# Two trunk layers in one launch: the opening modulation ahead of the tokens, and two projection tiles by turns

## The chip, the cores and the metric

The kernel runs on one core of one Trainium2 chip. TensorE (PE) does matmuls and transposes, VectorE (DVE), ScalarE (ACT) and GpSimd (POOL) do the work on vectors, SyncE (SP) issues the transfers in order. The metric is the device time of one launch in microseconds.

## The reference

One layer of a hybrid backbone is run for 1024 sample tokens and 256 prompt tokens that share all weights. Only the first part matters here:

```
mod = silu(cvec) @ w_mod + b_mod                 # (1024 x 6144)
sh1, sc1, g1, sh2, sc2, g2 = split(mod, 6)
h = rmsnorm(x, g_pre1) * (1.0 + sc1) + sh1
p = h @ w_in                                     # four head groups A, B, C, D
ya, yb, yc = short_conv(p[A]), gla(p[B], s0), chunk_mlp(p[C])
yd = hyena(p[D])                                 # row_conv3, then two long convolutions by FFT
x = x + g1 * rmsnorm(concat(ya, yb, yc, yd) @ w_out, g_post1)
x = x + g2 * rmsnorm(swiglu(rmsnorm(x, g_pre2) * (1 + sc2) + sh2), g_post2)
```

The filters of the long convolutions come from a small sine network (`filter_mlp`) and are taken to the frequency domain (`filter_spectra`).

## The kernel before

The 1280 tokens are three chunks: `CH = [(0, 512), (512, 512), (1024, 256)]`. Every large product runs as three products of a high and a low part: `mm3` does high weights by high tokens (L90), low tokens (L91) and low weights by high tokens (L92).

The opening, in `run`, makes the normalised, modulated and transposed tokens: `hh[n]` and `hl[n]`, the two parts of chunk n, eight blocks (`kt`) of 128 rows each.

- `mod_first(part)` is a generator with one step per 512 KB tile of w_mod: the transfer (L122) into one of seven buffers `s4`, which the `w_in` tiles and their parts use too, then four 32-column matmuls (L132) into one PSUM bank. With the fifth tile comes the bias (L129). Behind the eighth: copy (L135), two transposes (L138), copy (L140) and `mod_apply` (L378, L379), which writes the scale `sv` and the shift `bv`. Part 0 serves blocks 0 to 3 of every chunk, part 1 blocks 4 to 7. A buffer is free when the matmuls that read it are done, and the transfer into it waits for that on SP, with all transfers behind it.
- `norm1_rows(n)` loads 128 rows at a time (L388), squares them on ACT (L1609) and scales them by the root (L97, L98, L392).
- `chunk_hT(n, ..., kts)` transposes four such tiles per block (L401; two for chunk 2) into one of four banks `pm`, and `to_hT` empties it: ACT writes `hh` (L199), then DVE (L201) or ACT (L203) writes a full copy into one of two `tmp`, and POOL or DVE subtracts (L204) into `hl`.
- `load_w(ti)` loads a 512 KB tile of w_in (L83); ACT casts it to the high part (L65), DVE subtracts to the low part (L66). `later`, the second and third round of the modulation (L161, L164), takes a step with each call.
- `proj_d` makes six projection tiles (`ti`) for the long convolution, each for three chunks: 24 matmuls into a bank `pg`, a convolution (`conv3`: ACT L226, DVE L229 and L230), transposes into phases (L614, L618), a copy (L620) and a store to `xg` (L622).

Behind these come the products of `mixer_d` (`p`, L662 to L751, the FFTs), with projections of other head groups as fill, and `mixer_b`, whose chain begins with L924: two matmuls per chunk, ACT L925, L938, L940 over all chunks, and DVE's scans L944, L949. A scheduler sets the order on each engine from the program's order, its estimates and the buffers; so a change at the front moves rows far behind.

Of the kernel before, what the change touches and what calls it, by code (L numbers as in the profile page):

```python
# [20 lines left out]
KT = D // P  # L21
# [20 lines left out]
class Builder:  # L42
# [193 lines left out]
    def run(self):  # L236
        tc, nc, a = self.tc, self.nc, self.a
        with ExitStack() as ctx:
# [49 lines left out]
            with banks() as self.psm, sub("fl", side="right") as fl:  # L288
                h2 = fl.tile([P, T], F32R, name="h2")
                with sub("xs", side="right") as xs, sub("flm", side="right") as flm:  # L290
                    mod = [self.mod_first(0), self.mod_first(1)]
                    mlp = self.filter_mlp(flm, h2)
                    next(mod[0])
                    self.consts(const)
                    next(mlp)
                    for _ in range(2):
                        next(mod[0])
                    with tc.issue_after(self.mark.ins):
                        x = [self.norm1_rows(0, xs)]
                    for _ in mlp:  # L300
                        pass
                    for _ in mod[0]:
                        pass
                    self.chunk_hT(0, x[0], 0, self.pm, range(4))
                    next(mod[1])
                    with tc.issue_after(self.mark.ins):
                        x.append(self.norm1_rows(1, xs))
                    self.chunk_hT(1, x[1], 0, self.pm, range(4))
                    for _ in range(3):
                        next(mod[1])  # L310
                    with tc.issue_after(self.mark.ins):
                        x.append(self.norm1_rows(2, xs))
                    self.chunk_hT(2, x[2], 0, self.pm, range(4))
                    for _ in mod[1]:
                        pass
                    with tc.issue_after(self.mark.ins):
                        w = self.load_w(0)
                    for n in range(3):
                        self.chunk_hT(n, x[n], 0, self.pm, range(4, KT))
                self.later = itertools.chain(self.mod_round(1), self.mod_round(2))  # L320
                with sub("flk", side="right") as flk:
                    self.filter_spectra(flk, h2)
# [265 lines left out]
    def proj_d(self, first):  # L588
        self.hyconv = self.cst.tile([P, 6, 3], F32, name="hyconv")
        self.nc.sync.dma_start(self.hyconv, self.a["hyconv"])  # L590
        pending = None
        for ti in range(6):
            w = self.load_w(ti) if ti else first
            for n in range(3):
                ps = self.proj_fm(w, n, -1 if n == 1 else 1)
                o = self.pj()
                self.conv3(o, ps, self.hyconv[:, ti, ::-1 if n == 1 else 1], n)
                if pending:
                    self.to_phases(*pending)
                pending = (o, ti, n)  # L600
                if (ti, n) == (5, 1):
                    rows = self.load_w(10)
        self.to_phases(*pending)
        return rows
# [1160 lines left out]
```

## Time and profile before

| | |
|---|---|
| median of 3 runs | 1603.81 us (1602.39 to 1604.59) |
| the profiled execution | 1604.68 us, its span 1602.9 us |
| PE busy | 94% of the span |
| DVE, ACT, POOL busy | 64%, 42%, 25% |
| mean granted clock of PE | 0.974 |

The span is what the trace covers; the rest of the execution's time lies around it. PE is busy nearly throughout except in the opening and in stretches around 240 to 600 us. So what the change is worth is to be read from those stretches, wait by wait.

### The profile page before, as it was taken

What the parts mean: (1) busy time and instruction counts of PE and PEld (TensorE: products, weight loads), DVE (VectorE), ACT (ScalarE), POOL (GpSimd) and SP (SyncE); (2) the same over time, 40 slices, a digit from 0 to 9 for tenths busy, and PEclk for the clock granted to TensorE, in tenths of its full rate; (3) what the DMA queues carried; (4) which work ended last, traced back from release to release, by engine and by line L of the source; (5) the groups of instructions that cost most, each with busy time, mean ns of one, the idle gap of its engine ahead of it and who ended that gap; (6) DMA issues with size and microseconds to landing.
All of it is one profiled execution on the core that took longest, in us unless ns stands there. A gap on an engine that the chain in (4) does not pass through costs nothing.

```text
span 1602.9 us, 23276 instructions
## 1 busy us (share of the span) xinstructions
PE 1500.1 (94%) x8517; PEld 1241.8 (77%) x8517; DVE 1027.6 (64%) x1752; ACT 666.5 (42%) x1218; POOL 399.3 (25%) x406
## 2 busy tenths in 40 slices
PE   5999998889889889998979999999999999999996
PEld 2688877878578667787868888888888887888885
DVE  6776559998278897544766556665566535544467
ACT  5754244554356766555432222222222213433352
POOL 1433216566124665442010110101001000000004
PEclk9899998899999999999989999999999999999998
DMA  9435463442823084561124334343344438755576
GB/s 331 141 113 162 129 219 94 134 145 75 269 77 101 21 266 135 171 224 56 60 83 151 116 112 143 128 141 119 121 135 132 126 103 257 241 178 172 168 245 250
DMA packets 163226, 242.17 MB, mean 151 GB/s; under 512 B 34613, under 2 KB 97407, under 8 KB 162984
## 3 DMA queue, kind: packets, MB, share of 16 engines
q1 hardware_dynamic: 163112, 240.69, 46.1%
q8 instruction: 67, 1.10, 0.3%
q14 instruction: 47, 0.39, 0.1%
HBM read 169.05 MB, written 71.58 MB: 150 GB/s over the span
## 4 chain that ended last, share of the span: by engine, by line
PE 58%; DVE 6%; DMA 3%; ACT 3%; issue 3%; POOL 2%; SPq 0%; DVEq 0%; POOLq 0%; ACTq 0%
PE pg L1381 17%; PE pm L1381 7%; PE pg L1543 7%; PE pm L1543 6%; PE pg L90 4%; PE pg L92 4%; PE pg L91 4%; PE pm L90 3%; PE pm L91 3%; PE pm L92 3%; DMA raw<-w2t 1%; DMA s<-in_wfm 1%; DVE e L1029 1%; DVE qbd L1036 1%; PE pm L401 1%
## 5 line engine op out<-in xcount | busy, mean ns | idle before, releaser
L90 PE MATMUL pg<-hh,s 128*128 128x512 f32 (+1 forms) x432 | 157.6, 366 | 3.9 <-ACT s L65 3.4
L92 PE MATMUL pg<-hh,s 128*128 128x512 f32 (+1 forms) x432 | 154.3, 361 | 6.7 <-DVE s L66 6.7
L66 DVE TENSOR_TENSOR op<-raw,op 128x1152 fp32r<-128x1152 f32 x69 | 93.6, 1357 | 101.2 <-ACT op L65 101.0
L91 PE MATMUL pg<-hl,s 128*128 128x512 f32 (+1 forms) x432 | 155.5, 360 | 0.6 <-POOL hl L204 0.6
L1358 POOL TENSOR_TENSOR sr<-s,s 128x512 f32<-128x512 f32 x20 | 25.8, 1292 | 449.8 <-DVE sr L1356 449.8
L65 ACT CAST op<-raw 128x1152 fp32r<-128x1152 f32 x69 | 80.1, 1161 | 134.2 <-PE pg L1543 67.6
L65 ACT CAST s<-s 128x1024 fp32r<-128x1024 f32 (+2 forms) x67 | 69.6, 1039 | 118.0 <-DMA s<-in_w 82.4
L1543 PE MATMUL pg<-op,op 128*128 128x512 f32 x372 | 115.1, 391 | 1.8 <-DVE op L66 1.8
L98 POOL TENSOR_TENSOR rs<-rs,mhalf 128x1 f32<-128x1 f32 x40 | 29.0, 728 | 351.4 <-DVE rs L97 348.2
L1381 PE MATMUL pg<-b1h,s 128*128 128x512 f32 x320 | 108.4, 400 | 8.1 <-ACT t L1388 8.1
L65 ACT CAST su<-sr 128x512 fp32r<-128x512 f32 x80 | 49.5, 620 | 149.9 <-PE pm L1381 55.5
L66 DVE TENSOR_TENSOR s<-s,s 128x1024 fp32r<-128x1024 f32 (+2 forms) x67 | 86.7, 1295 | 34.7 <-ACT s L65 21.4
L1381 PE MATMUL pg<-hh,su 128*128 128x512 f32 x320 | 107.3, 396 | 0.0
L1543 PE MATMUL pm<-op,op 128*128 128x512 f32 x338 | 104.5, 390 | 0.0
L92 PE MATMUL pm<-hh,s 128*128 128x256 f32 x352 | 99.5, 283 | 0.0
L91 PE MATMUL pm<-hl,s 128*128 128x256 f32 x352 | 99.5, 283 | 0.0
L90 PE MATMUL pm<-hh,s 128*128 128x256 f32 x352 | 99.4, 282 | 0.0
L90 PEld LDWEIGHTS pg<-hh,s 128*128 128x128 f32 x432 | 82.5, 191 | 19.9 <-ACT s L65 4.8
L92 PEld LDWEIGHTS pg<-hh,s 128*128 128x128 f32 x432 | 82.1, 190 | 20.4 <-DVE s L66 7.6
L91 PEld LDWEIGHTS pg<-hl,s 128*128 128x128 f32 x432 | 82.5, 191 | 12.5 <-POOL hl L204 0.9
L1386 DVE TENSOR_TENSOR t<-t,pg 128x512 f32<-128x512 f32 x60 | 41.2, 686 | 75.8 <-PE pg L1381 60.3
L1543 PEld LDWEIGHTS pg<-op,op 128*128 128x128 f32 x372 | 70.0, 188 | 16.8 <-DVE op L66 2.3
(393 smaller groups left out, 4162.7 us busy)
## 6 DMA issues: line engine op xcount, KB each, us to landing
s<-in_wmod SPq DMA_DIRECT2D x48, 512.0 KB, 5.3
raw<-actd SPq DMA_DIRECT2D x75, 320.0 KB, 3.5
s<-in_w SPq DMA_DIRECT2D x44, 512.0 KB, 3.8
actd<-t SPq DMA_DIRECT2D x60, 256.0 KB, 3.6
tmp<-in_w SPq DMA_DIRECT2D x44, 256.0 KB, 3.2
w2t<-tmp SPq DMA_DIRECT2D x44, 256.0 KB, 2.1
raw<-w2t SPq DMA_DIRECT2D x44, 256.0 KB
s<-in_wfm SPq DMA_DIRECT2D x18, 512.0 KB, 5.0
```

The source lines that it names most:

```text
L65: nc.scalar.copy(hi, src)
L66: self.cut = (eng or nc.vector).tensor_tensor(lo, src, hi.bitcast(F32), ALU.subtract).ins
L90: mm(ps, lh, rh, start=start, stop=False)
L91: mm(ps, lh, rl, start=False, stop=False)
L92: self.last = mm(ps, ll, rh, start=False, stop=stop).ins
L98: nc.gpsimd.tensor_tensor(out, out, self.mhalf[:, :cols], ALU.pow)
L401: self.nc.tensor.transpose(ps[:, t * P:(t + 1) * P], x[:, kt * P:(kt + 1) * P], self.ident)
L1029: nc.vector.tensor_tensor(ek[:, :, 0, :], rf, bf[:, :, 0, :], ALU.subtract)
L1358: pt(s3, a1[:, c], a2[:, c], ALU.subtract)
L1381: self.last = mm(ps, l[:, k], r[:, k], start=start and k == 0 and i == 0, stop=stop and k == 3 and i == 2, skip_group_check=True).ins
L1386: add = lambda out, x, y: nc.vector.tensor_tensor(out, x, y, ALU.add)
L1543: mm(ps, l, r, start=start and i == 0, stop=stop and i == 2, skip_group_check=True)
```

## The change

In `run`, both parts of the modulation now stand ahead of all transposes, the first weight tile's load behind them, and chunk 0 gets its eight blocks in one go before chunks 1 and 2. The rows of chunks 1 and 2 are loaded after the first weight tile is asked for. In `proj_d`, tiles 0 and 1 take turns by chunks; for that both weight tiles are held until chunk 2. Every engine has the same instructions as before, in another order.

```diff
                     for _ in mod[0]:
                         pass
-                    self.chunk_hT(0, x[0], 0, self.pm, range(4))
-                    next(mod[1])
-                    with tc.issue_after(self.mark.ins):
-                        x.append(self.norm1_rows(1, xs))
-                    self.chunk_hT(1, x[1], 0, self.pm, range(4))
-                    for _ in range(3):
-                        next(mod[1])
-                    with tc.issue_after(self.mark.ins):
-                        x.append(self.norm1_rows(2, xs))
-                    self.chunk_hT(2, x[2], 0, self.pm, range(4))
                     for _ in mod[1]:
                         pass
                     with tc.issue_after(self.mark.ins):
                         w = self.load_w(0)
-                    for n in range(3):
-                        self.chunk_hT(n, x[n], 0, self.pm, range(4, KT))
+                    self.chunk_hT(0, x[0], 0, self.pm)
+                    for n in (1, 2):
+                        with tc.issue_after(self.mark.ins):
+                            x.append(self.norm1_rows(n, xs))
+                    for n in (1, 2):
+                        self.chunk_hT(n, x[n], 0, self.pm)
...
         pending = None
-        for ti in range(6):
-            w = self.load_w(ti) if ti else first
-            for n in range(3):
-                ps = self.proj_fm(w, n, -1 if n == 1 else 1)
+        w = {0: first}
+        for ti, n in [(0, 0), (1, 0), (0, 1), (1, 1), (0, 2), (1, 2), *itertools.product(range(2, 6), range(3))]:
+                if ti not in w:
+                    w[ti] = self.load_w(ti)
+                ps = self.proj_fm(w[ti], n, -1 if n == 1 else 1)
```

In the changed kernel the lines behind `run` have numbers lower by six (L401 is L395 there), those behind `proj_d` by five (L924 is L919).

**On SP, the transfers behind the modulation's first part, before.** x are rows of tokens, s the buffers for weights.

```order
L388 DMA x_384<-in_x 128x1024
L388 DMA x_393<-in_x 128x1024
L388 DMA x_402<-in_x 128x1024
L388 DMA x_411<-in_x 128x1024
L122 DMA s_92_456<-in_wmod 128x2x512
L590 DMA hyconv<-in_hyconv 128x18
L833 DMA convw<-in_conva 128x6
L122 DMA s_93_462<-in_wmod 128x2x512
L122 DMA s_94_468<-in_wmod 128x2x512
L388 DMA x_474<-in_x 128x1024
L388 DMA x_483<-in_x 128x1024
L122 DMA s_115_520<-in_wmod 128x2x512
```

The same place in the changed kernel, from the last two of the eight w_mod tiles on:

```order
L122 DMA s_58_388<-in_wmod 128x2x512
L122 DMA s_59_394<-in_wmod 128x2x512
L382 DMA x_487<-in_x 128x1024
L382 DMA x_496<-in_x 128x1024
L83 DMA s_63_409<-in_wfm 128x1024
L382 DMA x_505<-in_x 128x1024
L382 DMA x_514<-in_x 128x1024
L382 DMA x_523<-in_x 128x1024
L382 DMA x_532<-in_x 128x1024
L83 DMA s_346_1531<-in_wfm 128x1024
```

The six transfers of rows went from between the w_mod tiles to behind them, four of them also behind the first weight tile.

**On ACT, up to the high part of the first weight tile, before** (junk is the square of a row tile, pm a bank of transposes, hh0 to hh2 the chunks).

```order
L1609 ACTIVATE junk_102_487,bms_101_486<-x_99_483 128x1024
L199 ACTIVATE hh1_131<-pm_89_447,bv_139,sv_138 128x512
L203 ACTIVATE tmp_87_443<-pm_86_438,bv_139,sv_138 128x512
L199 ACTIVATE hh2_132<-pm_103_492,bv_139,sv_138 128x256
L199 ACTIVATE hh2_132<-pm_106_499,bv_139,sv_138 128x256
L199 ACTIVATE hh2_132<-pm_109_506,bv_139,sv_138 128x256
L65 CAST s4_124_565<-s4_123_563 128x1024
```

The changed kernel, from the first bank that is emptied at all:

```order
L199 ACTIVATE hh0_130<-pm_66_415,bv_139,sv_138 128x512
L203 ACTIVATE tmp_67_420<-pm_66_415,bv_139,sv_138 128x512
L1604 ACTIVATE junk_97_500,bms_96_499<-x_94_496 128x1024
L199 ACTIVATE hh0_130<-pm_69_424,bv_139,sv_138 128x512
L199 ACTIVATE hh0_130<-pm_72_433,bv_139,sv_138 128x512
L199 ACTIVATE hh0_130<-pm_75_442,bv_139,sv_138 128x512
L65 CAST s4_64_411<-s4_63_409 128x1024
```

Before, eleven of the 24 high parts stood ahead of that cast; now four do, and twenty stand behind it.

**On PE, the last two of mixer_b's six opening products, before** (hh0 and s4_828: a projection tile of another head group with its weights).

```order
L164 MATMUL pg_734_3944<-s4_825_4702,csil_122 32x512 x2
L90 MATMUL pg_830_4714<-hh0_130,s4_828_4710 128x512
L91 MATMUL pg_830_4714<-hl0_133,s4_828_4710 128x512
L90 MATMUL pg_832_4742<-hh1_131,s4_828_4710 128x512
L91 MATMUL pg_832_4742<-hl1_134,s4_828_4710 128x512
L90 MATMUL pg_834_4770<-hh2_132,s4_828_4710 128x256
L91 MATMUL pg_834_4770<-hl2_135,s4_828_4710 128x256
L924 MATMUL pm_805_4527<-gk_804_4525,wgk_sb_4497 128x256
L924 MATMUL pm_807_4532<-gk_804_4525,wgk_sb_4497 128x256
```

In the changed kernel the same six matmuls of pg_830 to pg_834 come first, and then 21 more of pg_830; the end of them and the pair:

```order
L92 MATMUL pg_830_4714<-hh0_130,s4_829_4711 128x512
L90 MATMUL pg_830_4714<-hh0_130,s4_828_4710 128x512
L91 MATMUL pg_830_4714<-hl0_133,s4_828_4710 128x512
L919 MATMUL pm_805_4527<-gk_804_4525,wgk_sb_4497 128x256
L919 MATMUL pm_807_4532<-gk_804_4525,wgk_sb_4497 128x256
L92 MATMUL pg_830_4714<-hh0_130,s4_829_4711 128x512
L92 MATMUL pg_832_4742<-hh1_131,s4_829_4711 128x512
```

So the pair moved behind 21 matmuls of 512 columns. By the same listing, 20 matmuls of pg_887 and pg_897 moved forward ahead of the next tile's products (pg_877) behind it. PE's first product of `mixer_d` (p) stands 26 matmuls later than before (7 of 512 columns, 15 of 256, 4 of the modulation), its last 47 later (45 of 512 columns, 2 of 256).

## Rows read from the trace of the kernel before

**Rows 1.** The page: busy time and share of an engine; clock in 40 slices.

```profile
PE 1500.1 (94%) x8517; PEld 1241.8 (77%) x8517; DVE 1027.6 (64%) x1752; ACT 666.5 (42%) x1218; POOL 399.3 (25%) x406
PEclk9899998899999999999989999999999999999998
```

**Rows 2.** Windows of the opening: from:to, length, busy per engine, clock, DMA share, GB/s.

```profile
32.00:38.00 6.00, 2.66 (x20) 2.18 (x21) 5.23 (x15) 5.97 (x13) 2.44 (x4) 1.00 1.04 393
...
41.00:44.80 3.80, 2.07 (x9) 1.22 (x7) 3.07 (x4) 2.13 (x5) 1.67 (x2) 0.50 0.04 15
44.80:48.50 3.70, 3.63 (x36) 1.46 (x40) 2.18 (x5) 3.70 (x7) 1.78 (x2) 0.52 0.34 82
...
57.00:72.00 15.00, 14.07 (x78) 11.35 (x77) 12.39 (x16) 12.85 (x22) 6.00 (x5) 1.00 0.37 121
```

**Rows 3.** Timeline of SP: start, duration, line, transfers; waits count in the duration.

```profile
31.53 14.85 SPq L122 DMA_DIRECT2D s<-in_wmod  x5
```

**Rows 4.** DMA issues, 40 to 60 us: tile, count, size, median us to landing.

```profile
s<-in_wmod SPq DMA_DIRECT2D x3, 512.0 KB, 4.2
```

**Rows 5.** Timeline of PE in the opening: start, duration, instruction, idle before it.

```profile
28.47 3.28 PE L132 MATMUL pm<-s,csil 128*32 128x256 f32 x26
...
44.87 3.62 PE L132 MATMUL pm<-s,csil 128*32 128x256 f32 x32 [0.22 <-ACT tmp L203]
...
52.07 0.64 PE L132 MATMUL pm<-s,csil 128*32 128x256 f32 x8
...
60.90 0.60 PE L401 MATMUL pm<-ident_sb,x 128*128 128x128 f32 x4
61.25 0.48 PE L91 MATMUL pg<-hl,s 128*128 128x512 f32 x1
...
94.61 0.50 PE L90 MATMUL pg<-hh,s 128*128 128x512 f32 x1
94.95 0.39 PE L91 MATMUL pg<-hl,s 128*128 128x512 f32 x1
95.18 0.40 PE L92 MATMUL pg<-hh,s 128*128 128x512 f32 x1
```

**Rows 6.** Timelines of ACT and DVE in the opening.

```profile
32.40 1.05 ACT L1609 ACTIVATE junk<-x 128x1024 bf16<-128x1024 f32 x1
33.36 0.18 ACT L1609 ACTIVATION_READ_ACCUMULATOR junk<-x 128x1 f32 x1
...
53.01 0.41 DVE L135 COPY pj<-pm 128x256 f32<-128x256 f32 x1
...
57.62 0.78 ACT L203 ACTIVATE tmp<-pm,bv,sv 128x512 f32<-128x512 f32 x1
58.28 0.78 ACT L199 ACTIVATE hh<-pm,bv,sv 128x512 fp32r<-128x512 f32 x1
58.94 1.05 ACT L65 CAST s<-s 128x1024 fp32r<-128x1024 f32 x1
```

**Rows 7.** PE, 96 to 222 us: line, what it waited for, total, times, longest.

```profile
PE pg L618 <- DVE pj L230: 1.3, 1, 1.3
```

**Rows 8.** Windows of mixer_d and of mixer_b (480:520), columns as in the second group.

```profile
240.00:280.00 40.00, 32.23 (x197) 30.70 (x195) 37.01 (x76) 20.42 (x67) 26.42 (x20) 0.88 0.32 94
...
360.00:400.00 40.00, 35.83 (x261) 34.39 (x263) 35.20 (x79) 19.21 (x62) 27.77 (x21) 0.91 0.25 73
...
480.00:520.00 40.00, 40.00 (x450) 32.76 (x443) 32.09 (x69) 25.17 (x56) 18.92 (x29) 1.00 0.33 106
```

**Rows 9.** Chain of waits, 404 to 480 us: start, duration, what.

```profile
441.46 0.43 PE pg L91
...
443.17 1.50 PE pm L924 x4
...
469.79 1.24 DVE s L66
```

**Rows 10.** PE, 440 to 520 us: what it waited for, as above.

```profile
PE pg L92 <- DVE s L66: 4.5, 1, 4.5
```

## The prediction, as put down before the changed kernel ran

> **What bounds the kernel now.** The page first: PE is busy for 94% of the span, DVE for 64%, and the clock row reads 9 nearly throughout [rows 1]. A gain can then only come from stretches in which PE waits, or in which it runs at half clock. The windows of the opening show one: from 41 to 44.8 us PE is busy 2.07 of 3.8 us, its clock is at 0.50, and the transfers do 15 GB/s after 393 shortly before [rows 2]. SP says why: five tiles of w_mod take it from 31.53 to 46.4, most of it waiting [rows 3]. The last of them waits for a buffer that only the first matmuls of the modulation's second part free, and these stand on PE behind the transposes of chunks 0 and 1, at 44.87 [rows 5]; the transposes in turn wait for ACT and DVE to empty four banks. So the second part ends at 52.71, 21 us after the first (31.75) [rows 5]. From 57 on PE is all but full: 14.07 of 15 us [rows 2], and tile 2 of the projections starts at 94.61 [rows 5]. Later, PE has idle time again in `mixer_d`: 32.2 of the first and 35.8 of the last 40 us between 240 and 400, while DVE is busy 37.0 and 35.2 [rows 8].
>
> **The opening, step by step.** The modulation's second part has 64 records on PE, 8 for a tile. Four tiles took 3.62 us, and 26 records of the first part 3.28 [rows 5], so about 0.95 us for a tile. In the changed kernel nothing stands between the parts. The first tile is done at about 32.9, the eighth can be asked for then or, with SP's queue, at about 33.9, and lands 4.2 us later [rows 4], at 38. PE by itself needs 8 x 0.95 and half a us for the bias: 41.0. That is the later one. At 393 GB/s [rows 2] the transfers keep up. The modulation is through 11.7 us earlier (52.71 - 41.0).
>
> Work that moves behind this point: twelve banks of transposes, eight of four (0.35 us: 60.90 to 61.25 [rows 5], or 0.4 where two follow each other) and four of two (0.2): 3.8 us. Work that moves behind tile 2's start: eight 512-column and ten 256-column matmuls of the spectra, at 0.23 us (94.95 to 95.18 [rows 5]) and half of it: 3.1 us. From the modulation's end to tile 2's start PE took 94.61 - 52.71 = 41.9 us, of which it idled 1.9 in its rows; 40.0 us of work. The changed kernel has 40.0 + 3.8 - 3.1 = 40.7, so without a wait tile 2 starts at 81.7. With the 3.1 us taken off on the side of before (91.5), the change gains 9.8 us, less its new waits. These are:
>
> - *The first weights.* L135, L138, L140 and the scale take 1.6 us before (53.01 to about 54.6 [rows 6]); so the first bank can be emptied at 42.6. On ACT stand then a high part (0.66: 57.62 to 58.28 is the same step of a copy), a copy 0.66, a square with its read 1.18 (32.40 to 33.58), three high parts 2.0 and the cast 1.0 [rows 6]: 48.1. By then the weight tile, third behind w_mod at 1.35 us a transfer (512 KB at 393 GB/s), has been there for long (42). PE has six banks and L138 to do in that time, 2.7 us of 7.1. New wait: 4.4 us.
> - *The low weights.* DVE's subtraction takes 1.24 us [rows 9]; the first two products cover part: 0.8 us.
> - *Single low parts and the first convolution*, which stand on ACT and DVE between evacuations: 0.6 and 1.2 us. ACT has about 30 us of such work from 42 to 75 (24 high parts and twelve copies at 0.66 or, for 256 columns, less; five squares, two casts), and DVE as much with the subtractions, hardly less than PE has. I take no more than these two, as in the window from 57 to 72 DVE and ACT are busy 12.4 and 12.9 of 15 us [rows 2] and PE waits for 0.9 only.
> - *The clock.* Before, PE's clock was 0.52 from 44.8 to 48.5, in which it worked almost without a pause, and 1.00 in the window from 57 [rows 2]. Now it works on transposes and waits from 41 to 48.1, so the first products run at half clock: 0.43 us for one [rows 9] against 0.23. If nine do, 1.8 us; part lies in the waits above, and I take 0.9.
>
> The Trainium skill says in "TensorE: Matmul & The Clock Gate", Part 4, that transposes don't count as PE-busy for the clock as matmuls do. The window from 41 to 44.8, transposes and waits at half clock, agrees but can't part the two causes. By that page the full 1.8 us would be due, and the sum below would be 0.9 us worse.
>
> Sum of the waits: 4.4 + 0.8 + 0.6 + 1.2 + 0.9 = 7.9; bounds 5.5 (the convolution and half of the first wait's excess hidden) to 8.8. Tile 2 starts at 89.6, and the opening gains **1.9 us** (1 to 4.3).
>
> **What follows.** Both weight pairs are held until chunk 2 is through, so tile 2's parts come, by the order, about when PE wants them, and the stores of the first two banks stand on SP ahead of the filter tables, so that these are asked for later while PE wants them earlier: I take 0.5 us lost (0 to 1.5, one wait of the kind and size of the one below). PE's one wait of 1.3 us between 96 and 222 [rows 7] may go with the new order: 0.6 gained (0 to 1.3).
>
> **mixer_d.** Its first product stands behind 26 more matmuls (7 of 512 columns, 15 of 256, 4 of the modulation at 0.11, as in the first part: 3.9 us), its last behind 47 (45 x 0.23 + 0.24 = 10.5 us). The work of PE as a whole is the same, so what lies ahead of it costs nothing, and 6.6 us of matmuls are put between its products. There PE idles 7.8 us in the first 40 and 4.2 in the last, some 24 of 160 by these two, and DVE is at 88 to 93% [rows 8]. If DVE is the bound, all 6.6 us go into idle time and are gained; if the chain of PE, ACT and DVE is bound by latency with PE in it, none. I take half, **3.0 us** (0 to 6.6), as neither engine is full.
>
> **mixer_b.** The third pair of its opening products stands behind 21 more matmuls, 4.8 us, and with it the whole chain to the scans. Behind it PE waited 4.5 us for a low part that stands on DVE behind the scans [rows 10]. But 20 other matmuls moved ahead of that wait, 4.6 us: the wait stays as it is. I take 0.5 us lost (0 to 4.9).
>
> Sum: 1.9 - 0.5 + 0.6 + 3.0 - 0.5 = 4.5 us faster. From the profiled execution's 1604.68 us (span 1602.9) that is 1600.2; the median of the runs is 0.9 us lower, and I predict **1599.3 us** for the median after.
>
> **Rivals.** *No change:* `mixer_d` takes the added matmuls on its path. Then 1.9 - 0.5 + 0.6 - 0.5 = 1.5 us are left, 1602.3; with the opening at its low bound and the spectra's waits at 1.5 it is 1604.2. For it speaks that ACT and DVE have nearly as much work in the opening as PE, and now start it later; against it, that DVE leads in `mixer_d`.
>
> *Slower:* the pair for `mixer_b`. If ACT's and DVE's chain (26.6 us from the pair at 443.17 to the start of the low part that PE waited for [rows 9]) is what sets the end there, 4.8 us come on top, and the 20 matmuls ahead only fill a longer wait: 1602.3 + 4.8 = 1607.1. It decides where PE has less than 4.5 us of other work before it needs the scans. Against it: from 480 to 520 PE is full [rows 8], so what it did earlier it need not do there.
>
> *More:* DVE is the bound of `mixer_d`, and all 6.6 us hide: 1603.81 - 8.1 = 1595.7; with the opening at its upper bound 1593.3.
>
> **How the numbers follow.** Chances: the forecast (1597.5 to 1601.5) 0.38, more (below) 0.20, no change (up to 1606) 0.29, slower 0.13. For 8 in 10 the range goes from the upper gain, 1593.5, to 1605.5, short of the slower case. 0.2% is 3.2 us, which is about what a measurement can tell from no change, so 1600.6 and 1607.0 are the borders: of the forecast's 0.38 some 0.3 lie below the first; with the 0.20, faster 0.50. Of the slower case two parts in three end above 1607.0: 0.09, and 0.03 for what I have not seen. Same: 0.38.
>
> **What would show it right or wrong.** The second part of the modulation should end near 41 us, not 52.7; the first L90 should start at about 48 with a wait for ACT's cast before it, at half clock; tile 2 should start between 87 and 91. PE's first product of `mixer_d` should come at the time of before within 2 us, its last not more than 5 us later, and the pair's scans should end about 5 us later against the products around them. It is wrong if PE waits for high or low parts all through 50 to 87 us (then ACT and DVE bound the opening, and it gains nothing), if `mixer_d` gets longer by all it was given, or if the wait for the low part at 471 us grows to 9 us.

## The result, and the profile after

The changed kernel takes 1617.2 us (median of 4 runs, 1614.5 to 1619.0) against 1604.0 us before in the same session: 1.0079 times as long, 95% interval 1.0061 to 1.0096. By this ratio it is 12.7 us slower (the medians lie 13.2 us apart), where 4.5 us faster was forecast, and above the range, which ended at 1605.5. The experiments below ran in other sessions, so differences between two runs are taken from their ratios to the kernel before. The profiled execution's span is 1615.1 us after 1602.9.

The windows of the changed kernel (from:to, length, then busy time and instructions of PE, weight load, DVE, ACT and POOL, PE's clock, DMA share, GB/s); the first seven answer to the opening in [rows 2], the last two to [rows 8]:

```profile
32.00:38.00 6.00, 3.94 (x64) 1.32 (x53) 1.65 (x6) 1.10 (x2) 0.00 (x0) 0.94 1.03 354
...
41.00:44.80 3.80, 3.78 (x21) 3.54 (x19) 2.08 (x7) 3.00 (x7) 0.67 (x2) 0.59 1.03 413
43.00:44.00 1.00, 1.00 (x6) 1.00 (x5) 0.59 (x2) 1.00 (x2) 0.00 (x0) 0.50 1.04 410
44.00:45.00 1.00, 0.78 (x7) 0.54 (x5) 0.26 (x2) 1.00 (x4) 0.32 (x1) 0.95 1.01 397
44.80:48.50 3.70, 1.71 (x6) 0.85 (x6) 2.59 (x3) 3.70 (x6) 1.70 (x2) 0.87 1.02 410
48.50:52.70 4.20, 3.54 (x12) 2.88 (x12) 3.09 (x6) 4.20 (x8) 2.25 (x3) 0.50 0.51 160
...
57.00:72.00 15.00, 13.61 (x73) 11.06 (x72) 11.30 (x16) 9.37 (x17) 6.91 (x6) 1.00 0.11 39
...
240.00:280.00 40.00, 34.57 (x216) 32.34 (x215) 39.00 (x76) 19.24 (x59) 24.85 (x20) 0.91 0.34 103
360.00:400.00 40.00, 34.01 (x264) 32.76 (x263) 38.79 (x83) 19.25 (x68) 26.14 (x21) 1.00 0.31 96
```

The hole in the transfers is gone (413 GB/s from 41 to 44.8, 15 before). But ACT did 1.10 us of work from 32 to 38, where it had done 5.97, and is full from 44.8 to 52.7. PE's timeline (start, duration, instruction, and in brackets the idle time before it) shows the steps that were forecast, the one that wasn't, and the end of mixer_d:

```profile
40.35 0.69 PE L138 MATMUL pm<-ident_sb,pj 128*128 128x128 f32 x2 [0.55 <-DVE pj L135]
40.83 3.95 PE L395 MATMUL pm<-ident_sb,x 128*128 128x128 f32 x20
46.79 0.66 PE L395 MATMUL pm<-ident_sb,x 128*128 128x128 f32 x4 [2.02 <-DVE tmp L201]
47.41 0.73 PE L90 MATMUL pg<-hh,s 128*128 128x512 f32 x1
...
49.82 0.63 PE L90 MATMUL pg<-hh,s 128*128 128x512 f32 x1
50.25 0.63 PE L91 MATMUL pg<-hl,s 128*128 128x512 f32 x1
...
91.65 0.30 PE L613 MATMUL pg<-ident_sb,pj 128*128 128x128 f32 x1 [2.08 <-DVE pj L230]
91.88 1.94 PE L164 MATMUL pg<-s,csil 128*32 128x512 f32 x8
93.74 0.80 PE L90 MATMUL pg<-hh,s 128*128 128x512 f32 x1
...
440.22 1.91 PE L164 MATMUL pg<-s,csil 128*32 128x512 f32 x12
442.59 1.96 PE L919 MATMUL pm<-gk,wgk_sb 128*128 128x512 f32 x4 [0.46 <-DMA gk<-gkd]
450.31 1.92 PE L164 MATMUL pg<-s,csil 128*32 128x512 f32 x4 [5.76 <-DMA s<-in_wmod]
```

The modulation is through by 40.35 (41.0 forecast). The first product starts at 47.41 (48), at half clock (0.43 us from 49.82 to 50.25). But tile 2 starts at 93.74 instead of 89.6: ahead of it PE waits 2.08 us for a convolution, and then runs at half clock again (eight records of the modulation in 1.94 us, which took 1.06 before at 93.62). ACT, then DVE, show behind what that convolution stood:

```profile
85.49 0.62 ACT L65 CAST fdfth<-st 128x512 fp32r<-128x512 f32 x1 [0.60 <-DMA st<-in_fdft]
86.12 1.28 ACT L529 ACT_TABLE_LOAD   x1
87.52 0.63 ACT L529 ACTIVATE el<-el 128x512 f32<-128x512 f32 x1
88.28 1.05 ACT L65 CAST s<-s 128x1024 fp32r<-128x1024 f32 x1
89.23 0.47 ACT L226 ACTIVATE pj<-pg,hyconv 128x256 f32<-128x256 f32 x1
```

```profile
89.36 1.23 DVE L66 TENSOR_TENSOR s<-s,s 128x1024 fp32r<-128x1024 f32 x1 [2.17 <-ACT s L65]
90.50 0.48 DVE L229 SCALAR_TENSOR_TENSOR pj<-pg,hyconv,pj 128x255 f32<-128x255 f32 x1
91.02 0.48 DVE L230 SCALAR_TENSOR_TENSOR pj<-pg,hyconv,pj 128x255 f32<-128x255 f32 x1
```

The convolution (L226, L229, L230) stands behind the cast and the low part of tile 2's weights, and these behind a filter table that came late. SP shows why: two stores to xg, which wait for ACT, take it until 81.36, and the tables are asked for behind them.

```profile
70.92 10.44 SPq L617 DMA_DIRECT2D xg<-pj  x2
81.41 0.92 SPq L476 DMA_DIRECT2D st<-in_fdft  x2
```

The last low part of the opening stands on POOL; in the changed kernel, then before:

```profile
84.66 0.74 POOL L204 TENSOR_TENSOR hl<-tmp,hh 128x256 fp32r<-128x256 f32 x1 [3.24 <-DVE tmp L201]
```

```profile
72.54 0.75 POOL L204 TENSOR_TENSOR hl<-tmp,hh 128x256 fp32r<-128x256 f32 x1 [0.16 <-DVE tmp L201]
```

The emptying of the 24 banks ends 12.1 us later than before. Last, the waits of PE from 433 to 470 us (before, 1.6 and 1.4 us):

```profile
PE pg L164 <- DMA s<-in_wmod: 5.8, 1, 5.8
PE pm L919 <- DMA gk<-gkd: 0.9, 2, 0.5
```

Over the opening as a whole PE is busy for as long as before. What differs is its clock (before, then the changed kernel):

```profile
20.00:100.00 80.00, 70.42 (x433) 48.65 (x434) 63.71 (x107) 58.92 (x99) 30.65 (x29) 0.94 0.59 203
```

```profile
20.00:100.00 80.00, 70.48 (x410) 48.84 (x411) 52.39 (x90) 52.72 (x87) 22.38 (x23) 0.89 0.55 193
```

To see where the time goes in each kernel, PE's records were weighted by the mean spacing of their kind. For the sum of work that the kernel before has done at a time in the head of the table, a row says how much later the other kernel has done as much (offset at 20 us taken off; negative is earlier). The weights are means, so a difference under about 1.5 us says nothing.

```
lag in us at     50     70     90    100    230    400    440    480    560    700
after          -5.5    1.0    3.0    4.1    8.2    8.2   15.9   13.0   15.0   13.8
e_open         -4.9    3.8   12.7   13.0   14.8   15.8   14.3   12.1   13.6   13.9
e_turns        -0.3   -0.4    5.9    5.3    9.5    9.2    7.8    6.2    6.1    3.3
e_late         -4.5    2.1    4.1    5.2    9.5    9.7   15.5   12.0   10.9    7.2
e_tab          -6.5    0.4    2.4    2.0    6.1    6.1   11.7    8.5    8.1    8.7
e_early        -8.1   -4.5   -2.5   -1.4    3.3    3.5    9.9    8.0    8.1    5.0
e_mid          -5.2   -2.9   -3.5   -0.7    0.0    0.0   -1.5   -1.5   -1.7   -2.0
e_light        -5.3   -4.4   -3.5   -3.2    1.3    1.5    8.3    5.5    4.8    5.4
e_light_b      -1.6   -2.2   -2.9   -2.6   -2.6   -2.9   -4.4   -5.2   -4.3   -6.5
```

The changed kernel is 5.5 us ahead at 50, has lost all of it by 70, is 4.1 behind at 100 and 15.9 at 440 (its own time is 455 there, behind the wait of 5.76 us). The 4.1 us at 100 are about what the clock makes: 0.94 less 0.89 is 0.05, and 0.05 of 80 us is 4.

From 100 to 230 it loses another 4 us with PE busy throughout but for one wait (1.0 us, 1.3 before). Most of that is in the later rounds of the modulation (L164). Their 56 records between 97 and 237 us take 8.91 us of PE before and 11.61 in the changed kernel, at full clock in both (columns: PE, weight load, clock, DMA share, GB/s):

```profile
97.00:237.00 140.00, 8.91 (x56) 1.65 (x56) 1.00 0.51 158
```

```profile
97.00:237.00 140.00, 11.61 (x56) 1.62 (x56) 1.00 0.49 151
```

The order breaks them into smaller groups, and a small group takes as long as a large one. Here are eight together (before) and two alone (changed kernel):

```profile
146.14 1.06 PE L164 MATMUL pg<-s,csil 128*32 128x512 f32 x8
```

```profile
108.26 1.04 PE L164 MATMUL pg<-s,csil 128*32 128x512 f32 x2
```

In e_mid (below) 54 of them take 8.45 us in this window, and its lag grows by 0.7 us only between 100 and 230. No run changes the grouping alone, so this is read from the traces and not tried. From 85 to 700 us the 128 records of L164 take 26.48 us instead of 19.96, some of it at half clock.

### The profile page after: what moved, and what is told of

It is laid out like the page before. It is cut to its first block, busy times and chain, and to the rows that moved or that the text cites. A ratio compares the mean times of both kernels' runs of the same rounds, so it can differ in the third digit from the quotient of the medians.

```text
span 1615.1 us, 23256 instructions
## 1 busy us (share of the span) xinstructions
PE 1507.7 (93%) x8517; PEld 1237.6 (77%) x8517; DVE 1030.3 (64%) x1752; ACT 666.7 (41%) x1218; POOL 397.4 (25%) x406
## 4 chain that ended last, share of the span: by engine, by line
PE 56%; DVE 7%; DMA 3%; issue 3%; ACT 3%; POOL 2%; SPq 0%; POOLq 0%; DVEq 0%; ACTq 0%
PE pg L1376 17%; PE pm L1376 7%; PE pg L1538 6%; PE pm L1538 6%; PE pg L90 3%; PE pg L91 3%; PE pg L92 3%; PE pm L90 3%; PE pm L91 3%; PE pm L92 3%; DMA raw<-w2t 1%; DVE qbd L1031 1%; DMA gk<-gkd 1%; DVE e L1027 1%; POOL acc L1647 1%
## 5 line engine op out<-in xcount | busy, mean ns | idle before, releaser
L90 PE MATMUL pg<-hh,s 128*128 128x512 f32 (+1 forms) x432 | 160.1, 371 | 3.1 <-DVE mvec L190 1.7
L92 PE MATMUL pg<-hh,s 128*128 128x512 f32 (+1 forms) x432 | 156.7, 365 | 3.6 <-DVE s L66 3.6
```

Of the source, the lines that this page charges most:

```text
L90: mm(ps, lh, rh, start=start, stop=False)
L92: self.last = mm(ps, ll, rh, start=False, stop=stop).ins
```

## The experiments

Two theories were there at first: the order of the opening costs the time (ACT and DVE start to empty banks later), or the turns do (two weight pairs held, convolutions and stores in another order).

**Each part alone.** `e_open` keeps the new opening and makes the tiles one by one; `e_turns` is the reverse, the old opening with the turns.

```diff
-        w = {0: first}
-        for ti, n in [(0, 0), (1, 0), (0, 1), (1, 1), (0, 2), (1, 2), *itertools.product(range(2, 6), range(3))]:
-                if ti not in w:
-                    w[ti] = self.load_w(ti)
+        for ti in range(6):
+            w = self.load_w(ti) if ti else first
+            for n in range(3):
```

> The new opening with the six projection tiles one by one as before. If the opening itself loses (ACT and DVE, which empty the transposes, start later and bound it), this run is slower than before by most of the 13 us, 1612 to 1617 us. If the loss comes from tiles 0 and 1 taking turns and from what the order does at the end of mixer_d, where this variant has no matmul of pg_816 to pg_820 ahead of mixer_d's last transposes (before 0, changed 47), it is within 4 us of before: 1600 to 1608, and PE's first L924 comes at 426 to 431 us.

> The opening as before, tiles 0 and 1 take turns. Here too no matmul of pg_816 to pg_820 stands ahead of mixer_d's last transposes. If the turns as such cost (filter tables behind the first stores, both weight pairs held), 1607 to 1612; if the loss needs both parts of the change, by the order that only both give at the end of mixer_d, 1602 to 1607; if the opening is the cause, 1604 as before.

Measured: e_open 1618.5 us, 1.0082 [1.0066, 1.0098]; e_turns 1611.0 us, 1.0038 [1.0026, 1.0051]. Each part alone makes the kernel slower, by 13.2 and 6.1 us, and the two together (12.7) are not worse than the opening by itself. In e_open PE loses 9 us between 70 and 90, in this wait (PE, 41 to 97 us) and at half clock behind it:

```profile
PE pg L612 <- DVE pj L230: 5.4, 1, 5.4
```

On the new opening the turns take that wait away (9.7 us less lag at 90), and bring a later one (next). So the theory that the turns are what costs the time there fell. On the old opening they do cost 6.1 us, as that theory had it.

**The end of mixer_d.** Only with both parts do 47 matmuls of a later projection tile stand ahead of mixer_d's last transposes (none before, in e_open or in e_turns). The loads for mixer_b need mixer_d's memory, so they start later (the first, of wgk_sb, is asked for at 438.74 us, before at 418.83), and PE waits from 444.6 on for a tile of w_mod that SP asks for among them, at 443.03. `e_late` puts the tile behind these transposes.

```diff
-                nc.tensor.transpose(pt[:, kt * P:(kt + 1) * P], y2[:, kt, 4, :], self.ident)
+                self.dlast = nc.tensor.transpose(pt[:, kt * P:(kt + 1) * P], y2[:, kt, 4, :], self.ident).ins
...
-        self.proj_rows(self.load_w(8), self.qd, AF.Identity, 32.0 ** -0.5)
+        w8 = self.load_w(8)
+        with self.tc.issue_after(self.dlast):
+            self.proj_rows(w8, self.qd, AF.Identity, 32.0 ** -0.5)
```

> The changed kernel, but the projections of pg_816 to pg_820 are ordered on PE behind mixer_d's last two transposes, so that the loads of mixer_b's tensors, which need mixer_d's memory, have the same 47 matmuls to hide behind as before. Theory of the tail: the wait of 5.8 us for w_mod and the two for gk (0.9) go, mixer_d ends earlier, and the time falls by 5 to 8 us to 1609 to 1612. If the 47 matmuls only move and the end is bound elsewhere: 1615 to 1618.

Measured: 1611.9 us, 1.0042 [1.0027, 1.0057], 6.0 us less than the changed kernel. Its waits of PE from 433 to 470 us:

```profile
PE pm L919 <- DMA gk<-gkd: 2.3, 1, 2.3
PE pg L90 <- ACT s L65: 0.7, 1, 0.7
```

The wait of 5.8 us is gone and the time falls by as much, so the order of these 47 matmuls is a cause. How it costs the time is not shown. The loads for mixer_b are asked for at 439.15 us in a trace that begins 2.3 us later, so some 2 us earlier at most; the lag at 440 is what it was (15.5), and the gain comes between 480 and 620. By which work inside mixer_b it comes was not found.

**The tables behind the stores.** `e_tab` puts the first store of tiles 0 and 1 on SP behind the filter tables; `e_opentab` does so without turns, `e_tablate` together with e_late.

```diff
-            nc.sync.dma_start(el, a["ld"][o:o + 1].to_broadcast([P, 512]))
+            ld = nc.sync.dma_start(el, a["ld"][o:o + 1].to_broadcast([P, 512]))
+            if o == 0:
+                self.tab = ld.ins
...
-        nc.sync.dma_start(xg[:, n, 0:4, :] if n < 2 else xg[:, :, 4, :], sg[:, :N].rearrange("p (d c) -> p d c", c=P))
+        with self.tc.issue_after(self.tab) if ti < 2 and n == 0 else nullcontext():
+            nc.sync.dma_start(xg[:, n, 0:4, :] if n < 2 else xg[:, :, 4, :], sg[:, :N].rearrange("p (d c) -> p d c", c=P))
```

> The changed kernel, but on SP the stores of the first two banks of tiles 0 and 1 stand behind the loads of the filter tables. Theory of the queue: the tables land some 20 us earlier, ACT's cast of weight tile 2 does not stand behind a table that has not landed, the wait of 2.1 us before tile 2 and the half clock behind it go; the time falls by 2 to 4 us to 1613 to 1615. If PE would have waited there for the weights or the convolution anyway, under 1 us of difference.

> The new opening, tile by tile (e_open, 1618.5 us), but on SP the first store of phases stands behind the loads of the filter tables. In e_open PE waited 5.4 us at 86.6 for a convolution that stood on DVE behind low parts of tables and taps, and then ran 13 matmuls at half clock. Theory of the queue: the tables land some 15 us earlier, the wait and the half clock go, 6 to 8 us: 1610 to 1612.5. If ACT and DVE are late anyway because all 24 evacuations start at 42 us: less than 2 us of gain, 1616.5 or more.

> The changed kernel with both orders: tables ahead of the first stores, and pg_816 to pg_820 behind mixer_d's transposes. If the two losses are separate, their gains (3.8 and 5.2 us) add up: 1607 to 1610. If e_tab's gain was that of the tail by chance (its lead over the changed kernel came behind 440 us in its trace), no more than e_late: 1611 to 1613.

Measured: e_tab 1613.4 us, 1.0057 [1.0042, 1.0071], 3.6 us less than the changed kernel; e_opentab 1618.6, 1.0088 [1.0073, 1.0102], no gain on e_open; e_tablate 1607.9, 1.0015 [1.0005, 1.0026], 10.3 us less than the changed kernel, about the sum of the two. In e_opentab the tables are asked for at 58.1 instead of 76.3, and PE waits all the same:

```profile
91.97 0.45 PE L614 MATMUL pg<-ident_sb,pj 128*128 128x128 f32 x1 [5.09 <-DVE pj L230]
```

So the queue was not what held e_open's convolution; the theory fell there. In both, SP's transfer of the bias into a `tmp` buffer, which waits for the last emptying, comes at 81.5 (72.94 before), and hw weights behind it. With turns the order on SP counts for some: e_tab's interval overlaps that of the changed kernel, but e_tablate is 4.3 us below e_late, and their intervals do not overlap. It is not by the wait that was named, though. In e_tab the convolution still comes late, now because ACT's cast of tile 2's weights waits for the pair that is held until chunk 2, and PE waits 2.08 us before tile 2 as in the changed kernel; only the half clock behind it is absent (ACT, then PE):

```profile
89.29 1.05 ACT L65 CAST s<-s 128x1024 fp32r<-128x1024 f32 x1 [1.02 <-PE pg L91]
```

```profile
92.66 0.30 PE L615 MATMUL pg<-ident_sb,pj 128*128 128x128 f32 x1 [2.08 <-DVE pj L230]
92.89 1.06 PE L164 MATMUL pg<-s,csil 128*32 128x512 f32 x8
```

By what the gain comes stays open.

**An earlier start of the emptying.** `e_early` transposes the first four blocks of chunk 0 between the two parts of the modulation, where they stood before; the rest stays as changed. `e_eopen` is that without turns.

```diff
                     for _ in mod[0]:
                         pass
+                    self.chunk_hT(0, x[0], 0, self.pm, range(4))
                     for _ in mod[1]:
                         pass
...
-                    self.chunk_hT(0, x[0], 0, self.pm)
+                    self.chunk_hT(0, x[0], 0, self.pm, range(4, KT))
```

> The changed kernel, but the first four blocks of chunk 0 are transposed between the two parts of the modulation, as before; nothing else. Theory of the evacuation: ACT idled from 34 to 40 us in the changed kernel and then was full from 42 to 57; with four banks (about 5 us of ACT and DVE) emptied while w_mod loads, PE's lead at 60 us (none in the changed kernel) becomes 2 to 4 us, and the time 1613 to 1615. If the filter tables set the end of the opening, nothing changes: 1616 to 1618.

> The new opening tile by tile (e_open, 1618.5 us), with the first four blocks of chunk 0 transposed between the two parts of the modulation (as in e_early). Theory of the evacuation: the low parts end earlier than in e_open (81 us) by 2 to 5 us, and with them the filters' weights on SP, which wait for the buffer tmp; the time falls by 8 to 12 us, as it did from the changed kernel to e_early: 1606 to 1610. If the gain of e_early came from the turns (PE has the second tile to go on with), 1615 to 1618.

Measured: e_early 1606.3 us, 1.0009 [1.0001, 1.0018], 11.2 us less than the changed kernel where 2 to 4 were expected; e_eopen 1610.7, 1.0039 [1.0026, 1.0051], 6.9 less than e_open. Windows and POOL's last low part of e_early:

```profile
36.00:42.00 6.00, 4.97 (x78) 2.43 (x71) 4.79 (x6) 2.77 (x4) 2.76 (x2) 1.00 0.73 248
...
57.00:72.00 15.00, 15.00 (x81) 12.56 (x82) 11.80 (x15) 10.18 (x17) 5.96 (x6) 1.00 0.15 52
...
20.00:100.00 80.00, 71.21 (x435) 49.84 (x436) 57.93 (x97) 54.38 (x91) 26.50 (x26) 0.96 0.58 203
```

```profile
79.73 0.74 POOL L204 TENSOR_TENSOR hl<-tmp,hh 128x256 fp32r<-128x256 f32 x1 [1.60 <-DVE tmp L201]
```

Four of 24 banks are emptied earlier, the last low part comes 4.9 us earlier, and PE is full from 57 to 72. That a late start of ACT's and DVE's work costs much of the time is borne out, with the turns and without them. In the opening itself it is 5.5 us (the lag at 100 is -1.4 after 4.1), most of it clock (0.96 after 0.89 from 20 to 100). The rest of the 11.2 us shows in the lags only behind 440 and is not explained.

**A shorter emptying.** The same theory by another way: `e_light` writes the low part in one step of DVE, without the copy and POOL's subtraction, in the opening alone; it leaves the shift out of the low part, so it computes something else and serves for its time only. `e_light_b` does that to the kernel before.

```diff
-    def to_hT(self, ps, cols, hi, lo, svec, bvec):
+    def to_hT(self, ps, cols, hi, lo, svec, bvec, short=False):
...
+        if short:
+            nc.scalar.activation(hi, ps, AF.Identity, bias=bvec, scale=svec)
+            nc.vector.scalar_tensor_tensor(lo, ps, svec, hi.bitcast(F32), ALU.mult, ALU.subtract)
+            return
```

> The changed kernel with less work in emptying the opening's banks: the low part is made by DVE in one step from the bank and the high part, without the copy on ACT or DVE and without POOL's subtraction; the shift is left out of the low part. ACT has 12 steps of 0.45 to 0.66 us less, and no buffer tmp is used, so that SP doesn't wait for one. Theory of the evacuation: the low parts end 6 us or more earlier than in the changed kernel (84.7 us), PE keeps a lead of 3 us or more at 70 us instead of a lag of 1, and the time falls by 6 to 10 us, to 1607 to 1611 (the tail's loss stays if the order there does). If weights, tables or the clock bound the opening, less than 3 us.

> The kernel before with the same shorter emptying (the shift is left out of the low part): the control. In the kernel before eleven high parts are done before the modulation's second part ends, so emptying should be worth less there than in the changed kernel: 0 to 4 us, 1600 to 1604. If it gains as much as e_light does over the changed kernel, the emptying is no more the changed kernel's trouble than it was before.

Measured: e_light 1605.0 us, 1.0004 [0.9991, 1.0017], 12.1 less than the changed kernel; e_light_b 1595.8, 0.9942 [0.9923, 0.9961], 9.3 less than before. The control gained more than was expected of it, so in the total only 2.8 us tell the kernels apart. In the lag at 100 us they are apart: the short emptying is worth 7.3 us there in the changed kernel and 2.6 in that of before, and with it the new opening is even with the old one (0.6 us ahead, less than the lags can tell), where it had been 4.1 behind. What the control gains after 230 us stays open.

**All together.** `e_tle` joins e_tab, e_late and e_early. `e_mid` also loads the rows of chunk 1 behind the second part's first tile. `e_midopen` is e_mid's opening, tile by tile, without e_tab and e_late.

> All three: tables ahead of the stores, pg_816 to pg_820 behind mixer_d, four blocks of chunk 0 between the parts of the modulation. If the three losses are separate and each is as large as its own run says, 1604 to 1607; if the order of mixer_d and mixer_b decides the rest, 1608 to 1612.

> e_tle, and the rows of chunk 1 are loaded behind the first tile of the modulation's second part, as before, so that ACT squares them while it has nothing to empty. Theory of the evacuation: ACT has four squares less between 42 and 57 us, the evacuations end 2 to 4 us earlier than in e_tle (80.5 us), and the time falls to 1598 to 1602, below the kernel before. If w_mod comes later by the four transfers (5.4 us) and the second part ends that much later, nothing is gained: 1602 to 1606.

> e_mid's opening, but the six projection tiles one by one and no other order changed. If the turns are worth something once the evacuations start early, this is slower than e_mid by 2 us or more; if they only cost weights and stores, it is as fast or faster.

Measured: e_tle 1603.4 us, 0.9989 [0.9976, 1.0002]; e_mid 1602.2, 0.9990 [0.9980, 1.0001]; e_midopen 1605.3, 0.9998 [0.9987, 1.0010]. All three are even with the kernel before: what the change lost can be had back, 14.5 us in e_tle where the three gains by themselves make 20.8, and none of the three is faster than the kernel before by more than can be measured. In e_mid the last low part comes 4.4 us earlier than in e_tle (76.16 after 80.54), as was expected of it, and nothing is gained by that. The turns, with their two repairs, are worth some 1.3 us (e_mid against e_midopen), within the intervals.

## Why the prediction was wrong

**Right:** the modulation's end, the first product and its half clock, and that the filter tables would be asked for late.

**The terms that failed first** are "The clock", of which the prediction took 0.9 us, and "Single low parts and the first convolution", at 0.6 and 1.2 ("I take no more than these two"). Up to the first product the forecast held: 7.1 us from the modulation's end, and 7.1 were measured (40.35 to 47.41). From there to tile 2 it took 46.3 us instead of 41.5:

```profile
47.40:93.75 46.35, 42.21 (x227) 33.85 (x226) 33.89 (x47) 35.76 (x61) 18.88 (x18) 0.91 0.31 99
47.40:54.35 6.95, 6.29 (x19) 4.77 (x19) 5.84 (x8) 6.95 (x11) 4.58 (x5) 0.51 0.47 161
91.85:93.75 1.90, 1.90 (x10) 0.21 (x9) 1.57 (x3) 1.26 (x5) 0.87 (x1) 0.51 0.84 244
```

PE idles 4.1 us there, where 2.6 were forecast: 0.66 for the low weights (forecast 0.8), 1.39 between 57 and 72 for banks and a convolution (0.6 for low parts), and 2.08 for the convolution before tile 2 (1.2). And it works some 8 us at half clock, which by the two windows costs about 4.0 us (an estimate: half of that work), where 0.9 was taken. The prediction counted nine products and put half of their 1.8 us into the waits. Nine did run so, but so did the transposes between them and the eight records behind the convolution. So about 3 us of the miss are clock and 1.5 are waits. Tile 2 came 4.1 us later than forecast, and the opening, which was to gain 1.9 us, is 4.1 behind at 100.

Behind both terms stands one reading. The prediction looked at the window from 57 to 72, where PE is nearly full before, and took from it that ACT and DVE keep up. They kept up because their 30 us of work began at 35.08 (the first high part before); in the changed kernel it begins at 41.93, and their last low part comes 12.1 us later. Between the first product and 100 us the clock fell twice, at 47.5 and at 91.9, and both times PE had just waited 2.0 and 2.1 us for DVE. e_early and e_light, which start that chain earlier or shorten it, are 5.5 and 7.3 us better at 100.

Of the 17 us between forecast and result the lags put about 6 on the opening, 4 on 100 to 230 us, 3 on mixer_d and 5 on what lies behind 400.

**Spectra and slots** (0.5 lost, up to 1.5): the transfers did come late, and the other order on SP takes about 4 us off with the turns. But PE's wait before tile 2 stays in e_tab, so that the tables cost it is not shown. PE's one wait between 96 and 222 [rows 7] became 1.0 us from 1.3, where 0.6 was to be gained. What this stretch lost, about 4 us, is mostly the grouping of the modulation's records. The prediction priced such a record at 0.11 us (in mixer_d), which holds in large groups only.

**mixer_d** (3.0 gained): nothing was hidden. From its first product at 221.85 to its last at 415.53 it took 193.7 us; now 204.1, from 232.6 to 436.7, 10.4 longer for 6.6 us of matmuls put in, and the lag from 230 to 400 stays at 8.2. DVE is busy 39.0 and 38.8 of 40 us there, after 37.0 and 35.2 [rows 8]: it was nearer to full than "neither engine is full" took it for, and the added matmuls bring emptying of their own. That the latter is the reason is argued from the windows, not tried.

**mixer_b** (0.5 lost): the scans start at 472.5 instead of 454.0, 18.5 us later, which is about 5 more than the lag around them, as forecast for the pair; and PE's 4.5 us [rows 10] did not grow into 9. That part held. What was not seen is the tile whose 47 matmuls moved ahead of mixer_d's last transposes. The prediction counted them as work that could hide and did not ask what waits for the end: the memory that mixer_d gives back, and the loads behind it, of which one kept PE waiting for 5.8 us. e_late prices the order of the 47 matmuls at 6.0 us; whether it is by these loads is not shown.

**The rule behind the clock.** The prediction gave the full 1.8 us for the nine products by the Trainium skill's "TensorE: Matmul & The Clock Gate", Part 4. They did run at half clock, but not for the page's reason, see the end.

Of the rivals the nearest is "No change", which named the cause ("ACT and DVE have nearly as much work in the opening as PE, and now start it later") and priced it at the opening's low bound of 1 us gained. All of the range took ACT and DVE for engines that follow PE.

## What to carry to other kernels

When a change takes the first work from an engine that has nearly as much to do as the bound one, price the whole of that engine's work from its new start, not only the first wait: here 7 us of idle ACT at the front came back as a chain that ended 12 us late. Read the clock beside the busy time: the opening lost its 4 us with PE as busy as before, at a mean clock of 0.89 after 0.94. Where matmuls are moved into a stage as cover, ask what is released at the stage's end (memory, buffers, loads), for it moves too: here the loads behind mixer_d were asked for 20 us later, with a lag of 8 us ahead of them. Two parts of a change are to be run alone and together: here the turns cost 6.1 us on the old opening, were 9.7 us ahead on the new one at 90 us, and had lost that again at 440, most of it at the end of mixer_d, where neither part alone moves the 47 matmuls.

## What the runs showed of the hardware

In the changed kernel the clock fell to half between 37 and 38 us, while PE waited for tiles of w_mod. PE did nothing but fp32 transposes against the identity from 41 to 44, at half clock, and the clock then rose to 0.95 (the windows 43 to 44 and 44 to 45 above) and stood high through a 2.0 us pause, behind which it fell. By the Trainium skill, "TensorE: Matmul & The Clock Gate", Part 4, transposes do not count as PE-busy for the clock in the way matmuls do; this trace does not agree, as the clock rose behind transposes alone, and it was behind the pause that it fell. A pause of 2.1 us at 90 was followed by half clock as well (1.94 us for the eight records), but the same pause in e_tab was not (1.06 us for the same eight).

A record of the modulation's 32-column matmuls has no fixed price: two alone took 1.04 us, eight together 1.06, both at full clock.

The first transfers land at times that differ by up to 2.9 us from one trace to another (PE's first record is at 8.4 us in e_light_b, 8.9 in the changed kernel, 10.1 before and 11.3 in e_late), which is why the lags are counted from 20 us on.
